# Two block products put between key projection and scores, with the rows for the block sums in another buffer

## The chip, the cores and the metric

The kernel runs on one core of a Trainium2 chip. The metric is device time in microseconds for one execution, from which a median over runs is taken. One execution of the kernel before was recorded by the hardware profiler; all its rows below are in microseconds from the start of its span, unless a column says ns. The engines are named as the profile names them: PE (TensorE, matmuls), DVE (VectorE), ACT (ScalarE), POOL (GpSimd), SP (SyncE, which issues most loads). PE multiplies, DVE and ACT do the element work.

## The reference, cut to what matters

The program is one layer of a hybrid model: 512 tokens, width 1024, float32. Branch A is a gated delta rule, branch B a retention with four heads; then a gate, an output projection and an MLP follow. The change touches branch B alone:

```python
proj = rmsnorm(x, n_mix_pre) @ w_in                     # qb, kb, vb, gb and more are columns of it
qb, kb = rotary(qb, pos), rotary(kb, pos) * 256 ** -0.5 # 4 heads, 256 wide
ob = chunk_retention(qb, kb, vb)                        # scores * decay @ vb, vb 512 wide a head
ob = rmsnorm(ob, norm_b) * silu(gb)
yb = ob.reshape(512, 2048) @ w_br_b                     # 512 rows of ob per head and 512 of w_br_b
```

So `yb` is a sum over the four heads of a (512 tokens x 512) by (512 x 1024) product.

## The kernel before, in words

Every float32 product is made of three matmuls. Each operand is split into a high half, a cast, and a low half, what the cast left over: `whi`/`wlo` for weights (L148 on ACT, L149 on DVE), `kr`, `qr`, `og`, `osum` for the others, each with a cast on ACT (`CAST`) and a subtraction on DVE. The three are high by high, high by low and low by high. A matmul group can start when the high halves are there, and needs the low ones a little later.

Weights come through a ring. SP loads a block of 128x1024 into a `raw` buffer (four of them), ACT and DVE split it into one of three `whi` and three `wlo` buffers, PE uses it. A split waits until PE has used up the buffer that it gets, three blocks back.

Branch B works head by head. The stage of head h runs in this order on PE:

- **Query and key projections**, 48 matmuls of 128x512 each (L93 to L95, two weight blocks for each, results in two banks of `mm` each; there are four `mm` banks in all, taken in turn).
- In the stages of heads 1 to 3, **transposes** (L402, four 128x128 in a group, results in the one bank `tr`) turn the output `o` of the head before, which stands by tokens, into features. `branch_quarters` makes from it the operands of the branch product.
- **Scores** of this head: four groups of keys by queries, 512, 384, 256 and 256 columns wide, into three banks `dl` in turn. DVE takes each from its bank with the decay factors (`sc`), and splits it (`s`).
- **The branch product of the head before**, in `branch_seven`: `o` times the 512x1024 block of `w_br_b`, done with seven half-size block products instead of eight. Three of them, "11", "12" and "22", take quarters of `o` as they are; four, "s1" to "s4", take sums and differences of quarters. Each is 12 matmuls of 128x512. The results are added to `acc` by DVE (for the first head some are copied there by ACT).
- **Values and gates** of this head, again with seven block products (`seven`), and the output `o`.

`rotary` takes a projection's two banks: four products with cosine and sine on DVE (L1541 to L1544, two for each bank), then a difference and a sum (L1545, L1546), then for each the cast (L1548, ACT) and the low half (L1549, DVE). Its result for the keys is `kr`.

Each engine works through its own instructions in a fixed order. That order is made when the program is built, by a scheduler that goes by the order of the code and by priorities (`tc.high_priority`). An instruction that waits holds up everything behind it on its engine.

In the kernel before, `branch_quarters` writes all four transposed feature groups as float32 into a tile `full`, which has the tag `kr`: it takes the same buffer as the keys' result `kr`, so a key cast can write only after everything has read `full`. All the sums and differences, and their halves (`osum`), are made there.

Of the kernel before, what the change touches and what calls it, by code (L numbers as in the profile page):

```python
# [10 lines left out]
F32 = mybir.dt.float32  # L11
# [8 lines left out]
P = 128  # L20
# [43 lines left out]
def hybrid_block_kernel(ctx: ExitStack, tc: tile.TileContext, a: dict, out: bass.AP):  # L64
# [1444 lines left out]
    with tc.tile_pool(name="pb", bufs=1) as pb_:  # L1509
# [41 lines left out]
        def scores(h, rows):  # L1551
# [3 lines left out]
            xq = branch_quarters(h - 1, rows) if rows else None  # L1555
# [4 lines left out]
            if h == 0:  # L1560
                ya_marks.append(ya_partial(3, prev))
            scs = []
# [23 lines left out]
            return scs, xq  # L1586

        def branch_quarters(h, rows):

            full = pb_.tile([P, 4, T], F32, tag="kr", name="full")  # L1590
            og = [act.tile([P, 4, T], F32R, tag="og", name="og") for _ in range(2)]
            sums = [pb_.tile([P, 2, 2, 2, 256], F32R, tag=f"vr{i}", name="osum") for i in range(2)]
            for f in range(4):
                ps = psx.tile([P, 4, P], F32, tag="tr", name="tr", bufs=1)
                for t in range(4):
                    transpose(ps[:, t, :], rows.feature(t, f))
                n = 4 * h + f
# [7 lines left out]
            xq = {}  # L1605

            def halved(name, src, pair):
                nc.scalar.copy(pair[0], src)
                nc.vector.tensor_tensor(pair[1], src, pair[0], ALU.subtract)
                xq[name] = pair  # L1610

            a11, a12, a21, a22 = (part(full, kh, th) for kh, th in ((0, 0), (1, 0), (0, 1), (1, 1)))
            for name, src, kh, th in (("11", a11, 0, 0), ("12", a12, 1, 0)):
                halved(name, src, [part(w, kh, th) for w in og])
            xq["22"] = [part(w, 1, 1) for w in og]
            nc.scalar.copy(xq["22"][0], a22)
            nc.vector.tensor_tensor(xq["22"][1], a22, xq["22"][0], ALU.subtract)
            nc.vector.tensor_tensor(a22, a21, a22, ALU.subtract)
            nc.vector.tensor_tensor(a21, a11, a21, ALU.subtract)
            nc.vector.tensor_tensor(a11, a22, a11, ALU.subtract)  # L1620
            nc.vector.tensor_tensor(a12, a12, a11, ALU.add)
            for i, src in ((2, a11), (1, a22), (3, a21), (4, a12)):
                w = sums[(i - 1) // 2][:, (i - 1) % 2]
                halved(f"s{i}", src, [w[:, 0], w[:, 1]])
            return xq

        def branch_seven(h, xq):
# [22 lines left out]
            a = bank(psx)  # L1650
# [6 lines left out]
            add(0, 0, b)  # L1657
            plus(v, x)
# [3 lines left out]
            c = bank(psm)  # L1662
# [13 lines left out]
        def outputs(h, scs):  # L1676
            vs = [pb_.tile([P, 4, T], F32R, tag=f"vr{i}", name="vr") for i in range(2)]
            gs = pb_.tile([P, 4, T], F32, tag="kr", name="gs")

            def value(t, p):  # L1680
                nc.scalar.copy(vs[0][:, t, :], p)
                nc.vector.tensor_tensor(vs[1][:, t, :], p, vs[0][:, t, :], ALU.subtract)
# [7 lines left out]
            for j in (3, 2, 1, 0):  # L1690
                ps = psx.tile([P, T], F32, tag="dl", name="dl", bufs=3)
                for i in range(j + 1):
                    js = slice((j - i) * P, (j - i + 1) * P)
                    mm3(
                        ps,
                        (scs[i][0][:, js], scs[i][1][:, js]),
                        (vs[0][:, i, :], vs[1][:, i, :]),
                        i == 0,
                        i == j,
                    )  # L1700
                nc.vector.tensor_tensor(o[:, j, :], ps, gs[:, j, :], ALU.mult)
                nc.scalar.activation(tmp("osq"), ps, AF.Square, accum_out=ss[:, j : j + 1])
# [21 lines left out]
        for h in range(4):  # L1724
            scs, xq = scores(h, rows)
# [12 lines left out]
            else:  # L1738
                branch_seven(h - 1, xq)
# [4 lines left out]
        for i in range(2):  # L1744
            ya.append(pb_.tile([P, 2, D], F32, tag=f"vr{i}", name="ya"))
            kept = nc.scalar.dma_start(ya[i], ya_d[:, 2 * i : 2 * i + 2, :])
            gates.append(pb_.tile([P, 2, D], F32, tag=("qr", "kr")[i], name="tb"))

        def gate_b(t, half, src):
            hs = slice(half * 512, half * 512 + 512)  # L1750
            tb = gates[t // 2][:, t % 2, hs]
            nc.scalar.activation(tb, src, AF.Tanh, scale=0.5)
            if t < 2:
                return
            m = acc_rows(t, half)
            nc.vector.scalar_tensor_tensor(m, tb, 1.0, m, ALU.add, ALU.mult)
            nc.vector.tensor_tensor(m, m, ya[t // 2][:, t % 2, hs], ALU.add)
# [10 lines left out]
        for pair in (1, 0):  # L1768
            pss = [[psm.tile([P, T], F32, tag="mm", name="mm") for _ in range(2)] for _ in range(2)]
            for i in range(2):  # L1770
                t = 2 * pair + i
                tt = slice(t * P, (t + 1) * P)
                for half in range(2):
# [7 lines left out]
                    if t < 2:  # L1781
                        rest, total = ya[t // 2][:, t % 2, hs], acc_rows(t, half)
# [334 lines left out]
```

## Time and profile before

| what | value |
|---|---|
| three runs | 1360.79, 1361.19, 1363.46 us |
| median | 1361.19 us |
| the profiled execution | 1362.24 us |
| its span, first to last instruction | 1359.8 us |
| PE busy | 1313.7 us, 97% of the span, 6555 matmuls |
| DVE busy | 971.4 us, 71% |
| ACT busy | 690.4 us, 51% |
| DMA | 231.01 MB, mean 170 GB/s |
| mean granted clock of PE | 0.987 |

The profiled execution has 2.4 us outside its span. A busy PE in this table counts matmuls from start to modelled end, which overlap; what a stage gains by is read from where PE stands idle, or from matmuls that start at a larger distance. The granted clock is the share of full speed that the chip allowed PE.

### The profile page before, as it was taken

The page shows a single profiled execution, that of the slowest core. Times are in us where ns is not written, and L with a number is a line of the kernel's source. Part 1 is how long each engine was busy: PE and PEld are TensorE (multiplying, and loading weights), DVE is VectorE, ACT ScalarE, POOL GpSimd, SP SyncE. Part 2 cuts the span into 40 slices and gives each one's busy share as a digit, 9 for nine tenths or more (in the row PEclk, how much of TensorE's full clock was granted, in tenths as well). Part 3 has the DMA queues.
Part 4 walks back from the last instruction along what each step waited for, and adds up shares of the span by engine and source line. Part 5 has one row for each costly group of instructions (what it writes and reads, how often), then busy time and mean ns, then how long its engine had stood idle before and what let it go on. Part 6 is the DMA issues. An engine that isn't in the chain of part 4 may idle for free.

```text
span 1359.8 us, 17583 instructions
## 1 busy us (share of the span) xinstructions
PE 1313.7 (97%) x6555; PEld 1085.3 (80%) x6555; DVE 971.4 (71%) x1614; ACT 690.4 (51%) x1198; POOL 96.1 (7%) x101
## 2 busy tenths in 40 slices
PE   9999999999999999997997997999999999999997
PEld 7888787888788788886886886888888888888786
DVE  6889767476466578967768868879775746738368
ACT  5783546555433424554554454455355737445364
POOL 2101100000000000010000000000002000001001
PEclk9999999999999999998998998999999999999999
DMA  5337843376675477991494561465629887959735
GB/s 182 135 109 188 199 111 92 96 195 188 179 176 145 93 229 178 267 262 53 150 257 76 149 219 45 140 202 170 224 88 227 223 234 178 268 163 243 211 110 138
DMA packets 118868, 231.01 MB, mean 170 GB/s; under 512 B 7222, under 2 KB 39136, under 8 KB 118272
## 3 DMA queue, kind: packets, MB, share of 16 engines
q1 hardware_dynamic: 98176, 179.85, 40.9%
q0 software_dynamic: 18576, 43.69, 19.8%
q10 hardware_dynamic: 2032, 6.36, 1.3%
q8 instruction: 51, 0.84, 0.2%
q14 instruction: 33, 0.27, 0.1%
HBM read 224.61 MB, written 78.66 MB: 223 GB/s over the span
## 4 chain that ended last, share of the span: by engine, by line
PE 76%; DVE 11%; ACT 6%; DMA 5%; issue 2%; ACTq 0%; DVEq 0%
PE mm L322 16%; PE mm L673 14%; PE dl L322 11%; PE mm L93 7%; PE mm L95 7%; PE mm L94 7%; PE dl L673 5%; DVE wlo L149 3%; DMA raw<-in_w_up_dram 2%; PE dl L93 2%; PE dl L94 1%; PE dl L95 1%; ACT whi L148 1%; PE tr L402 1%; DMA raw<-sums 1%
## 5 line engine op out<-in xcount | busy, mean ns | idle before, releaser
L148 ACT CAST whi<-raw 128x1024 fp32r<-128x1024 f32 x278 | 292.6, 1054 | 369.3 <-PE mm L322 90.1
L149 DVE TENSOR_TENSOR wlo<-raw,whi 128x1024 fp32r<-128x1024 f32 x278 | 339.9, 1223 | 195.0 <-ACT whi L148 194.4
L673 PE MATMUL mm<-actT,whi 128*128 128x512 f32 x448 | 144.5, 403 | 0.0
L322 PE MATMUL mm<-whi,xsum 128*128 128x512 f32 x384 | 120.5, 390 | 0.0
L93 PE MATMUL mm<-hn,whi 128*128 128x512 f32 (+1 forms) x288 | 106.3, 369 | 2.8 <-ACT r L1905 1.8
L95 PE MATMUL mm<-hn,wlo 128*128 128x512 f32 (+1 forms) x288 | 106.2, 369 | 0.5 <-DVE wlo L149 0.5
L94 PE MATMUL mm<-hn,whi 128*128 128x512 f32 (+1 forms) x288 | 105.9, 368 | 0.0
L673 PEld LDWEIGHTS mm<-actT,whi 128*128 128x128 f32 x448 | 80.6, 188 | 14.8
L673 PE MATMUL mm<-actT,wlo 128*128 128x512 f32 x224 | 87.8, 392 | 0.0
L322 PEld LDWEIGHTS mm<-whi,xsum 128*128 128x128 f32 x384 | 71.8, 188 | 14.9
L322 PE MATMUL mm<-wlo,xsum 128*128 128x512 f32 x192 | 74.8, 390 | 0.0
L322 PE MATMUL dl<-whi,ffq 128*128 128x512 f32 x224 | 71.3, 389 | 0.0
L93 PEld LDWEIGHTS mm<-hn,whi 128*128 128x128 f32 x288 | 54.7, 190 | 12.3 <-ACT r L1905 2.0
L95 PEld LDWEIGHTS mm<-hn,wlo 128*128 128x128 f32 x288 | 54.6, 190 | 9.9 <-DVE wlo L149 1.0
L673 PE MATMUL mm<-whi,og 128*128 128x512 f32 x192 | 62.3, 397 | 0.0
L673 PE MATMUL mm<-whi,actT 128*128 128x512 f32 x176 | 60.8, 407 | 1.0 <-DVE qf L907 1.0
L94 PEld LDWEIGHTS mm<-hn,whi 128*128 128x128 f32 x288 | 54.7, 190 | 8.8
L322 PE MATMUL dl<-whi,actT 128*128 128x512 f32 x192 | 61.1, 390 | 0.0
L322 PE MATMUL mm<-whi,ffq 128*128 128x512 f32 x192 | 60.9, 389 | 0.0
L1910 DVE TENSOR_TENSOR ffq<-r,ffq 128x512 fp32r<-128x512 f32 (+1 forms) x64 | 39.3, 623 | 28.0 <-ACT ffq L1910 27.8
L135 POOL DMA_DIRECT2D sums<-in_w_in_dram x28 | 32.7, 1167 | 336.7 <-DMA sums<-in_w_in_dram 336.5
L93 PE MATMUL mm<-actT,whi 128*128 128x512 f32 x128 | 51.5, 402 | 0.0
(426 smaller groups left out, 2877.2 us busy)
## 6 DMA issues: line engine op xcount, KB each, us to landing
raw<-in_w_in_dram SPq DMA_DIRECT2D x95, 512.0 KB, 4.7
raw<-sums SPq DMA_DIRECT2D x70, 512.0 KB, 4.9
raw<-in_w_up_dram SPq DMA_DIRECT2D x36, 512.0 KB, 6.5
sums<-in_w_in_dram SPq DMA_DIRECT2D x32, 512.0 KB, 5.8
sums<-in_w_down_dram SPq DMA_DIRECT2D x32, 512.0 KB, 6.8
sums<-in_w_in_dram POOLq DMA_DIRECT2D x28, 512.0 KB, 7.6
raw<-in_w_down_dram SPq DMA_DIRECT2D x24, 512.0 KB, 4.9
sums<-sums POOLq DMA_DIRECT2D x20, 512.0 KB, 8.2
```

The costliest lines, as they stand in the source:

```text
L93: nc.tensor.matmul(ps, lh, rh, start=first, stop=False)
L94: nc.tensor.matmul(ps, lh, rl, start=False, stop=False)
L95: nc.tensor.matmul(ps, ll, rh, start=False, stop=last)
L135: tc.keep_in_program_order(nc.gpsimd.dma_start(dst, src, accum_op=ALU.add))
L148: nc.scalar.copy(hi[:, :n], raw[:, :n])
L149: nc.vector.tensor_tensor(lo[:, :n], raw[:, :n], hi[:, :n], ALU.subtract)
L322: m = nc.tensor.matmul(pss[t], lhs[i // 2], rhs[i % 2], start=first and k + i == 0, stop=k + i == kts + 1, skip_group_check=not first,)
L402: nc.tensor.transpose(ps, src, ident)
L673: m = tc.keep_in_program_order(nc.tensor.matmul(*args, **kwargs))
L1910: return nc.scalar.copy(dst[0], r), nc.vector.tensor_tensor(dst[1], r, dst[0], ALU.subtract)
```

## The change

Four things are changed, and all concern the stages of heads 1 to 3.

1. **Another buffer.** The tile `full` is gone. Only the two upper feature groups are kept as float32, in `upper`, with a buffer of its own (tag `vr0a`, beside the values). The two lower groups are split straight from the transposes' bank into `og` by `split_from` (L387 on ACT, L388 on DVE). The values' two tiles `vr0`, `vr1` become four half-size tiles; the three other quarters of that room hold the sums. So `kr` no longer waits for readers of `full`.
2. **Two products earlier.** `branch_seven` becomes a generator. Its first part, the products "11" and "12", is called between key projection and scores; the rest runs after the scores. The banks are exchanged for it: the first product's results now go to `mm` banks, those of "s1" and "s4" to `dl` banks.
3. **Sums later.** The sums are made in `branch_sums`, called after the product "12". They start from `upper` alone, and read the lower quarters back from their halves (`xq["22"]`, `xq["12"]`), with an addition or subtraction for each half. "s4" takes the place of the unused quarter in `og`.
4. **Transposes earlier**, by `tc.high_priority(100)`.

Outside the stages, the load of `ya` at the end of branch B is made of four DMAs on ACT's queue instead of two, since it uses the split tiles.

```diff
@@ scores
-            xq = branch_quarters(h - 1, rows) if rows else None
+            parts = branch_quarters(h - 1, rows) if rows else None
...
             if h == 0:
                 ya_marks.append(ya_partial(3, prev))
+            else:
+                branch = branch_seven(h - 1, *parts)
+                next(branch)
             scs = []
...
-            return scs, xq
+            if h:
+                for _ in branch:
+                    pass
+            return scs
@@ branch_quarters
-            full = pb_.tile([P, 4, T], F32, tag="kr", name="full")
             og = [act.tile([P, 4, T], F32R, tag="og", name="og") for _ in range(2)]
-            sums = [pb_.tile([P, 2, 2, 2, 256], F32R, tag=f"vr{i}", name="osum") for i in range(2)]
+            upper = pb_.tile([P, 2, T], F32, tag="vr0a", name="upper")
             for f in range(4):
                 ps = psx.tile([P, 4, P], F32, tag="tr", name="tr", bufs=1)
-                for t in range(4):
-                    transpose(ps[:, t, :], rows.feature(t, f))
-                n = 4 * h + f
-                nc.scalar.activation(
-                    full[:, f, :], ps.rearrange("p t c -> p (t c)"), AF.Copy, scale=nb[:, n : n + 1]
-                )
+                with tc.high_priority(100):
+                    for t in range(4):
+                        transpose(ps[:, t, :], rows.feature(t, f))
+                ps, n = ps.rearrange("p t c -> p (t c)"), 4 * h + f
+                w = nb[:, n : n + 1]
+                if f < 2:
+                    nc.scalar.activation(upper[:, f, :], ps, AF.Copy, scale=w)
+                else:
+                    split_from(ps, og[0][:, f, :], og[1][:, f, :], w)
...
+            xq["s4"] = [part(w, 0, 1) for w in og]
+            a11 = upper[:, :, 0:256]
+            nc.scalar.copy(xq["11"][0], a11)
+            nc.vector.tensor_tensor(xq["11"][1], a11, xq["11"][0], ALU.subtract)
+            return xq, upper
+
+        def branch_sums(xq, upper):
+
+            sums = [pb_.tile([P, 2, 2, 256], F32R, tag=tag, name="osum") for tag in ("vr0b", "vr1a", "vr1b")]
...
+            a11, b = upper[:, :, 0:256], upper[:, :, 256:512]
+            nc.vector.tensor_tensor(b, a11, b, ALU.subtract)
+            halved("s3", b)
+            nc.vector.tensor_tensor(b, b, xq["22"][0], ALU.add)
+            nc.vector.scalar_tensor_tensor(b, b, -1.0, xq["22"][1], ALU.mult, ALU.subtract)
+            halved("s2", b)
+            nc.vector.tensor_tensor(a11, b, a11, ALU.add)
+            halved("s1", a11)
+            nc.vector.tensor_tensor(b, b, xq["12"][0], ALU.add)
+            nc.vector.tensor_tensor(b, b, xq["12"][1], ALU.add)
+            halved("s4", b)
@@ branch_seven
-            a = bank(psx)
+            a = bank(psm)
             times(a, "11", x, True)
             add(0, 0, a, new=True)
...
             times(b, "12", v, True)
             add(0, 0, b)
+            branch_sums(xq, upper)
+            yield
             plus(v, x)
             times(a, "s2", x, False)
...
-            c = bank(psm)
+            c = bank(psx)
             times(c, "s1", w, True)
@@ outputs, and the load of ya at the end
-            vs = [pb_.tile([P, 4, T], F32R, tag=f"vr{i}", name="vr") for i in range(2)]
+            pairs = [[pb_.tile([P, 2, T], F32R, tag=f"vr{i}{x}", name="vr") for x in "ab"] for i in range(2)]
...
-            kept = nc.scalar.dma_start(ya[i], ya_d[:, 2 * i : 2 * i + 2, :])
+            for j in range(2):
+                ya.append(pb_.tile([P, D], F32, tag=f"vr{i}{'ab'[j]}", name="ya"))
+                nc.scalar.dma_start(ya[-1], ya_d[:, 2 * i + j, :])
```

The order of instructions shows where the scheduler put things. First PE at the end of the key projection in the stage of head 2, before the change. `mm<-actT` are the last projection matmuls, `dl<-qr,kr` the scores of this head, `dl<-whi,og` the first matmul of the product "11".

```order
L94 MATMUL mm<-actT,whi 128x512
L95 MATMUL mm<-actT,wlo 128x512
L93 MATMUL dl<-qr,kr 128x512
L94 MATMUL dl<-qr,kr 128x512
L95 MATMUL dl<-qr,kr 128x512
```

The same place after it, where `mm<-whi,og` are the last matmuls of "12".

```order
L322 MATMUL mm<-whi,og 128x512 x2
L322 MATMUL mm<-wlo,og 128x512
L322 MATMUL mm<-whi,og 128x512
L93 MATMUL dl<-qr,kr 128x512
L94 MATMUL dl<-qr,kr 128x512
L93 MATMUL dl<-qr,kr 128x384
L94 MATMUL dl<-qr,kr 128x384
L93 MATMUL dl<-qr,kr 128x256
L94 MATMUL dl<-qr,kr 128x256
L95 MATMUL dl<-qr,kr 128x512
```

The 24 matmuls of two products now stand ahead of the first score. The scores themselves are interleaved: three groups do their first high-by-high and high-by-low matmuls before any does a low-by-high one (L95).

Next DVE in the same stage, before the change, from the keys' last two rotary products (L1543, L1544) to the first score taken from its bank (L1580).

```order
L1543 TENSOR_TENSOR ro<-mm,rope 128x512
L1544 TENSOR_TENSOR ro<-mm,rope 128x512
L149 TENSOR_TENSOR wlo<-raw,whi 128x1024
L1620 TENSOR_TENSOR full<-full 128x2x256
L1609 TENSOR_TENSOR osum<-full,osum 128x512
L1621 TENSOR_TENSOR full<-full 128x2x256
L1609 TENSOR_TENSOR osum<-full,osum 128x512 x3
L1545 TENSOR_TENSOR ro<-ro 128x512
L1546 TENSOR_TENSOR ro<-ro 128x512
L1549 TENSOR_TENSOR kr<-ro,kr 128x512 x2
L1580 TENSOR_TENSOR sc<-dl,dec 128x512
```

And after it, where `acc<-acc,mm` (L1658) adds a half of a finished product to `acc`, the first two of "11" and the next two of "12".

```order
L1543 TENSOR_TENSOR ro<-mm,rope 128x512
L1544 TENSOR_TENSOR ro<-mm,rope 128x512
L149 TENSOR_TENSOR wlo<-raw,whi 128x1024
L1658 TENSOR_TENSOR acc<-acc,mm 128x512 x2
L149 TENSOR_TENSOR wlo<-raw,whi 128x1024
L1658 TENSOR_TENSOR acc<-acc,mm 128x512 x2
L1545 TENSOR_TENSOR ro<-ro 128x512
L149 TENSOR_TENSOR wlo<-raw,whi 128x1024
L1546 TENSOR_TENSOR ro<-ro 128x512
L1549 TENSOR_TENSOR kr<-ro,kr 128x512
L1634 SCALAR_TENSOR_TENSOR upper<-upper,og 128x2x256
L1549 TENSOR_TENSOR kr<-ro,kr 128x512
```

The six rows of sums ahead of L1545 are gone; four additions to `acc` and a second and third weight split stand there or between. Behind them, up to the sums' low halves, come:

```order
L1636 TENSOR_TENSOR upper<-upper 128x2x256
L1583 TENSOR_TENSOR sc<-dl,dec 128x512
L1583 TENSOR_TENSOR sc<-dl,dec 128x384
L1583 TENSOR_TENSOR sc<-dl,dec 128x256
L1583 TENSOR_TENSOR sc<-dl,dec 128x128
L1628 TENSOR_TENSOR osum<-upper,osum 128x512 x2
```

The low halves of "s2" and "s1" (L1628) now follow all four scores. In the stage of head 1, where ACT copies "11" to `acc`, DVE has only the two additions of "12", and they stand behind L1545 and L1546; both low key halves follow them there.

More of the change, by code (lines that the diff above doesn't have):

```diff
@@ L1612, in branch_quarters @@
[L1612 to L1627, printed above, removed]
+            xq = {name: [part(w, kh, th) for w in og] for name, kh, th in (("11", 0, 0), ("12", 1, 0), ("22", 1, 1))}
+            xq["s4"] = [part(w, 0, 1) for w in og]
@@ L1724, in hybrid_block_kernel @@
         for h in range(4):
-            scs, xq = scores(h, rows)
+            scs = scores(h, rows)
             if h == 0:
@@ L1781, in hybrid_block_kernel @@
                     if t < 2:
[L1782 removed]
+                        rest, total = ya[t][:, hs], acc_rows(t, half)
                         nc.vector.tensor_tensor(total, total, pss[i][half], ALU.add)
```

23 lines of the change are left out of this document (11 added, 12 removed).

## The prediction

> **What bounds the kernel now.** I read the busy table first, then the waits of PE, then PE's timeline around the longest wait, then DVE's there, then windows of 3.41 us for the granted clock.
>
> ```profile
> PE 1313.7 (97%) x6555; PEld 1085.3 (80%) x6555; DVE 971.4 (71%) x1614; ACT 690.4 (51%) x1198; POOL 96.1 (7%) x101
> PE dl L93 <- ACT kr L1548: 23.3, 3, 7.8
> PE dl L673 <- ACT vt L1375: 2.9, 1, 2.9
> ```
>
> PE is busy for 97% of the span, so only what PE waits for, or does slowly, is time to be won. One wait towers over the rest: the first score waits for the keys' high half three times, 23.3 us in all; the next one on the list is 2.9 us. PE's timeline shows one of the three, and what follows it:
>
> ```profile
> 622.98 0.39 PE L94 MATMUL mm<-actT,whi 128*128 128x512 f32 x1
> 623.20 0.39 PE L95 MATMUL mm<-actT,wlo 128*128 128x512 f32 x1
> 631.37 0.80 PE L93 MATMUL dl<-qr,kr 128*128 128x512 f32 x1 [7.77 <-ACT kr L1548]
> 631.96 0.63 PE L94 MATMUL dl<-qr,kr 128*128 128x512 f32 x1
> 632.38 0.63 PE L95 MATMUL dl<-qr,kr 128*128 128x512 f32 x1
> 634.69 0.33 PE L93 MATMUL dl<-qr,kr 128*128 128x384 f32 x1
> 634.86 0.33 PE L94 MATMUL dl<-qr,kr 128*128 128x384 f32 x1
> 635.21 0.28 PE L93 MATMUL dl<-qr,kr 128*128 128x256 f32 x1
> 635.33 0.28 PE L94 MATMUL dl<-qr,kr 128*128 128x256 f32 x1
> 639.55 2.72 PE mm L322 x12
> ```
>
> A 512-column matmul starts 0.227 us after the last (2.72 for the 12 of a product) and lasts 0.39, so its result is out 0.16 after the next one's slot. 384 columns take 0.17, 256 take 0.12. Behind the wait, matmuls start 0.43 apart: the clock is down. The windows tell how long:
>
> ```profile
> 347.47:350.88 3.41, 0.60 (x3) 1.00 0.10 36
> 350.88:354.30 3.42, 3.42 (x10) 0.51 0.26 88
> 627.36:630.78 3.42, 0.00 (x0) 0.51 0.43 153
> 630.78:634.19 3.41, 2.83 (x7) 0.50 0.01 2
> 722.94:726.35 3.41, 1.74 (x8) 1.00 0.34 52
> 726.35:729.77 3.42, 0.00 (x0) 1.00 0.31 86
> 729.77:733.18 3.41, 0.74 (x2) 0.50 0.18 67
> 733.18:736.59 3.41, 3.41 (x11) 0.50 0.02 5
> 832.17:835.58 3.41, 1.45 (x4) 0.50 0.02 6
> 835.58:838.99 3.41, 3.41 (x11) 0.50 0.00 0
> ```
>
> Columns: window, its length, PE's busy time, granted clock. Behind a window in which PE was busy for 1.45 us or less stands one at half clock; behind 1.74 us stands a full one. In the three stages PE works 2.83, 0.74 + 3.41 and 1.45 + 3.41 us at half clock, 11.84 in all, and loses half, 5.9. With the waits, the three stages lose **29.2 us**, 9.7 each. That is all there is to win at this place.
>
> Why the keys are late, DVE's timeline tells:
>
> ```profile
> 621.04 0.69 DVE L1541 TENSOR_TENSOR ro<-mm,rope 128x512 f32<-128x512 f32 x1
> 622.24 1.22 DVE L1636 TENSOR_TENSOR raw<-raw 128x1024 f32<-128x1024 f32 x1
> 623.37 0.69 DVE L1619 TENSOR_TENSOR full<-full 128x512 f32<-128x512 f32 x1
> 628.11 1.89 DVE L1609 TENSOR_TENSOR osum<-full,osum 128x512 fp32r<-128x512 f32 x3
> 629.91 0.69 DVE L1545 TENSOR_TENSOR ro<-ro 128x512 f32<-128x512 f32 x1
> 630.51 0.69 DVE L1546 TENSOR_TENSOR ro<-ro 128x512 f32<-128x512 f32 x1
> 631.35 1.29 DVE L1549 TENSOR_TENSOR kr<-ro,kr 128x512 fp32r<-128x512 f32 x2
> ```
>
> DVE never pauses, and does the sums before the keys' difference. A 512-column row takes a slot of 0.60 and is out after 0.69; a 1024-column one 1.13 and 1.22.
>
> **The change, part by part.** All times from here count from the end of the key projection (0 is the slot after its last matmul).
>
> *Sums off the keys' path, two products into the gap.* Products "11" and "12" fill 0 to 5.44. The operands of "11" are early, and its banks are the queries', already read. So the scores can start at 5.44 if the keys are there. They are not, by DVE's new order. I lay it out with the slots above, and with these for ACT and the rest:
>
> ```profile
> 618.32 1.06 ACT L148 CAST whi<-raw 128x1024 fp32r<-128x1024 f32 x1
> 630.69 1.17 ACT L1548 CAST kr<-ro 128x512 fp32r<-128x512 f32 x2 [1.84 <-DVE ro L1545]
> L388 DVE SCALAR_TENSOR_TENSOR og<-tr,vecs,og x4: 743/747/751, 918.0 to 930.5; 128x512 fp32r<-128x512 f32 x4
> ```
>
> Stages of heads 2 and 3, on DVE: the second pair of key products 0.2 to 1.4, the split for "s2" to 2.5, the two additions of "11" to 3.7 (the second half of "11" is out at 2.9), the split for "s1" to 5.1, the first addition of "12" to 5.7, the second to 6.3 ("12" is out at 5.6). Only now L1545, to 7.0; ACT casts it, to 7.64. **First wait: 5.44 to 7.67, 2.23 us.** Six high-half score matmuls (1.03) end at 8.70; the low half comes after the split for "s3" (to 8.03), L1546 (8.63) and L1549 (9.32): **second wait, 0.65**. The fourth score group takes the first group's bank, which DVE reads after the second low half and L1636, until 11.72; PE is there at 11.43: **0.3**. "s2" starts at 12.47 and needs its low half at 12.92; DVE makes it only after the fourth score, at 13.64: **0.75**. Sum 3.95 a stage.
>
> Stage of head 1: ACT makes the copies of "11", so L1545 and L1546 come before all additions and the high keys are there by 5.4. The low half stands behind both additions of "12" and the split for "s1": 0.9. The second low half 0.2, the first bank for the fourth group 0.7 (the low half of "s2" stands ahead of its reader), the low half of "s1" 0.9, since six rows of sums and scores stand ahead. Sum 2.7.
>
> *Transposes earlier.* They move from the key to the query projection. There the first one stands 19 matmuls behind the start, at 599.51 + 4.31 = 603.82, and needs the normed output, which ACT begins at 603.55:
>
> ```profile
> 599.51 0.39 PE L93 MATMUL mm<-actT,whi 128*128 128x512 f32 x1
> 603.55 1.95 ACT L1707 ACTIVATE o<-o,rs_y 128x512 f32<-128x512 f32 x3 [2.42 <-DVE rs_y L383]
> 606.34 0.72 ACT L1707 ACTIVATE o<-o,rs_y 128x512 f32<-128x512 f32 x1
> 610.56 0.44 PE tr L402 x4
> ```
>
> The output is there at 604.3, so PE waits 0.5. I take 0.45 for it and the more frequent switching together; between nothing (the wait took the place of the one for `tr` before) and 1.0.
>
> *DVE and ACT work.* DVE has two rows more a stage (1.2 us) and ACT two casts less (1.0); both stand in the order laid out above, or later beside the values' products, where DVE has time to spare. The split of the values' tiles and two DMAs more at the end I cost at nothing: PE works on a gate's products there; without that cover it is one ACT issue each, under 1 us together. Loads on SP keep their order but for three weight copies, each exchanged with a neighbour: nothing, up to 1 us.
>
> *Sum.* Three times 0.45, 2.7 and twice 3.95 are 11.95 us of new waits. To these comes the clock. The first wait of the stages of heads 2 and 3 has PE idle for 2.1 us, which leaves 1.3 us of work if one window holds all of it, below the 1.45 that brought half clock, and more if it straddles two. One in two, so I count one slow window, with 1.2 us (half of 3.41 at most, less since part of it is waits anyway). 29.2 - 11.95 - 1.2 = **16.0 us gained**. The profiled execution took 1362.24, with 1359.8 of span and 2.4 around it, and would take 1346.2. It stood 1.05 over the median, so I say **1345.2**.
>
> The Trainium skill weighs the clock otherwise: "TensorE: Matmul & The Clock Gate", section "Why this matters for your kernels", wants idle gaps of more than about 3 us before the clock drops. The trace differs: a gap of 2.9 us at 347 was enough. By that page no slow window would be left, and the sum would be 1344.0.
>
> **Rivals.**
>
> *The gain is larger.* The new waits rest on DVE's order and on tenths. Where additions and casts meet PE a little earlier, the four later waits of a stage shrink. Speaking for it: none of them is over 1 us. Without them and without slow windows, the three stages keep 1.35 for the transposes, 0.9, and twice 2.9: 8.0 us; 1361.2 - 29.2 + 8.0 = 1340.0. With no wait left but the transposes', 1333.3. Against it: the first wait hangs on PE itself, as the second addition needs all of "12".
>
> *The clock swings.* Several waits of under 1 us after the first one keep PE under half busy, so that a window follows a window at half clock. For three windows a stage, 1.7 us each, the nine cost 15.4: 1361.2 - 29.2 + 11.95 + 15.4 = 1359.4, no change to speak of. Against it: between the waits lie 1.0 to 1.6 us of work each, and 1.74 us in a window held the clock up. The Trainium skill tells of such a swing on the same page, section "A second HAM failure mode: psum-queue depth-cycling", from short idle times between matmul groups. No window quoted above has one: each half clock stands behind a wait of over 2 us.
>
> *The wait only moves.* The change says that sums come later; if the products "s2" and "s1" then wait for them as the scores did, nothing is won. Ten rows of sums and halves at 0.60 would have to stand between scores and "s2", 6 us a stage, for 18: 1363. The new order has one or two there. That is the 0.75 and 0.9 above.
>
> *Slower.* "12" takes the keys' two banks, which L1541 to L1544 must have read. If DVE arrives late at the keys, "12" and with it the additions, L1545 and the scores move by as much. The three stages pay 4.0 each as laid out, against 9.7; it turns slower by more than can be told from 6.6 us of lateness in each. With 7.5: 1345.2 + 22.5 = 1367.7. For it:
>
> ```profile
> 618.00:624.00 6.00, 5.59 (x25) 4.31 (x23) 6.00 (x10) 2.60 (x4) 0.00 (x0) 1.00 0.00 0
> ```
>
> DVE (the third busy time) has no idle moment around the end of the key projection, and gets two rows more. Against it: the keys' first bank was done at 623.43 - 2.72 + 0.16 = 620.87, and DVE reached L1541 at 621.04, so its lateness came with the sums behind.
>
> **How the numbers follow.** Forecast as laid out, 1341 to 1350: 0.66. A larger gain, 1333 to 1341: 0.16. Clock or moved wait, 1352 to 1363: 0.12, half of it still faster. Slower by DVE's lateness or by something unseen: 0.06. The range takes in most of the larger gain, and upwards two more slow windows (2.4) and 0.3 us on each of the fifteen new waits (4.5): **1338 to 1352**. A change within 0.2%, 2.7 us, is about what a measurement of this kernel can't tell from none. Faster 0.89, same 0.06, slower 0.05.
>
> **What would show it.** In the waits of the changed kernel, "PE dl L93 <- ACT kr" falls from 23.3 to about 4.5, twice some 2.2 and near nothing in the stage of head 1; new rows with low halves come up, `kr` and `osum` on DVE, under 1 us each, and a transpose waiting for `o`, 0.5, three times. DVE's row L1545 stands directly behind the additions of "12" in two stages. The granted clock rises from 0.987 to about 0.993; the windows behind the scores' first wait show 0.50 in at most two stages. The prediction is wrong if the first wait is over 4 us, if DVE reaches L1541 later than the keys' first bank by more than 1 us, or if the rest of the program, above all values and gates behind the branch products, takes longer than before.

## The result and the profile after

The changed kernel takes **1344.99 us** (median of four runs, 1342.42 to 1349.35) against 1361.28 for the kernel before: ratio 0.988, 95% interval 0.985 to 0.991. Run again beside the later experiments it took 1342.43, ratio 0.987 (0.985 to 0.989). The forecast was 1345.2. The profiled execution took 1343.75, with a span of 1341.9.

The busy table of the changed kernel, and the top of the list of what PE waits for within the three stages (total, times, longest):

```profile
PE 1309.0 (98%) x6555; PEld 1078.0 (80%) x6555; DVE 972.6 (72%) x1620; ACT 685.3 (51%) x1192; POOL 96.5 (7%) x101
PE dl L93 <- ACT kr L1548: 4.3, 2, 2.2
PE dl L95 <- DVE kr L1549: 1.5, 3, 0.8
PE mm L322 <- DVE osum L1628: 1.0, 2, 0.5
PE tr L402 <- ACT o L1725: 1.0, 3, 0.3
PE dl L322 <- DVE osum L1628: 0.5, 1, 0.5
```

The wait of the scores for `kr` fell from 23.3 us to 4.3, and small waits came up, for low halves (`kr`, `osum`) and for the output `o` at the transposes. PE's timeline in the stage of head 2, from the last matmul of "12" to the product "s2":

```profile
721.18 0.39 PE L322 MATMUL mm<-whi,og 128*128 128x512 f32 x1
723.74 0.50 PE L93 MATMUL dl<-qr,kr 128*128 128x512 f32 x1 [2.17 <-ACT kr L1548]
725.43 0.80 PE L95 MATMUL dl<-qr,kr 128*128 128x512 f32 x1 [0.37 <-DVE kr L1549]
726.02 0.63 PE L93 MATMUL dl<-qr,kr 128*128 128x512 f32 x1
726.45 0.63 PE L94 MATMUL dl<-qr,kr 128*128 128x512 f32 x1
731.20 0.73 PE L322 MATMUL mm<-whi,osum 128*128 128x512 f32 x2 [0.51 <-DVE osum L1628]
```

And DVE there, where the keys' difference L1545 stands behind the additions of "12":

```profile
718.50 1.28 DVE L1658 TENSOR_TENSOR acc<-acc,mm 128x512 f32<-128x512 f32 x2
720.02 1.23 DVE L149 TENSOR_TENSOR wlo<-raw,whi 128x1024 fp32r<-128x1024 f32 x1 [0.23 <-ACT whi L148]
721.16 1.28 DVE L1658 TENSOR_TENSOR acc<-acc,mm 128x512 f32<-128x512 f32 x2
722.36 0.68 DVE L1545 TENSOR_TENSOR ro<-ro 128x512 f32<-128x512 f32 x1
722.96 1.22 DVE L149 TENSOR_TENSOR wlo<-raw,whi 128x1024 fp32r<-128x1024 f32 x1
724.09 0.68 DVE L1546 TENSOR_TENSOR ro<-ro 128x512 f32<-128x512 f32 x1
```

The key projection's last slot ends at 715.97, so L1545 starts 6.4 behind it, and the score 7.77 behind it. At 726.02 and 726.45 matmuls start 0.43 apart: half clock again, for one window of 3.41 us. The windows of this stage and of the next (window, length, busy times of PE, PEld, DVE, ACT and POOL, granted clock, DMA share, GB/s):

```profile
721.65:725.06 3.41, 1.32 (x6) 1.02 (x6) 3.41 (x6) 1.87 (x3) 0.00 (x0) 1.00 0.98 267
725.06:728.47 3.41, 3.04 (x9) 2.67 (x9) 2.12 (x4) 1.61 (x3) 1.17 (x1) 0.50 0.86 193
817.23:820.64 3.41, 2.10 (x10) 1.40 (x8) 3.17 (x5) 1.56 (x2) 0.00 (x0) 1.00 0.65 171
820.64:824.05 3.41, 2.17 (x10) 1.75 (x11) 3.41 (x6) 1.51 (x3) 0.00 (x0) 1.00 0.97 330
824.05:827.46 3.41, 2.95 (x18) 2.22 (x16) 3.13 (x7) 2.60 (x6) 0.00 (x0) 1.00 0.54 114
```

Behind the wait of head 2, nearly all idle time falls into one window, which has 1.32 us of work; the next one is at half clock. In head 3 the same wait straddles two, 2.10 and 2.17 us of work are left, and the clock stays up.

**Where the time went, by stage.** This table is worked out from PE's timelines. A is query and key projection, B from their end to the first score, C the scores, D from there to the first product of scores with values (in it the rest of the branch product, the values and the gate's products). Each is the sum over the stages of heads 1 to 3. Without any wait A would be 71.8, C 11.5 (3 x 3.82), B 0 and D 171.4, or 16.3 and 155.1 with two products in B.

| kernel | A | B | C | D | sum | median us | ratio to before |
|---|---|---|---|---|---|---|---|
| before | 71.8 | 23.8 | 17.3 | 171.4 | 284.4 | 1361.28 | 1 |
| changed | 73.1 | 21.0 | 17.1 | 157.7 | 268.9 | 1344.99 | 0.988 |
| late sums only | 73.1 | 11.8 | 18.4 | 171.5 | 274.8 | 1349.92 | 0.993 (0.991 to 0.995) |
| products only | 71.8 | 37.9 | 19.7 | 155.1 | 284.5 | 1355.99 | 0.996 (0.994 to 0.998) |
| gap filled | 71.8 | 23.8 | 11.9 | 171.5 | 279.0 | 1354.09 | 0.995 (0.992 to 0.997) |
| late additions | 73.1 | 19.9 | 13.2 | 160.1 | 266.3 | 1342.59 | 0.987 (0.985 to 0.990) |
| "s4" early | 73.1 | 19.9 | 14.7 | 156.6 | 264.3 | 1337.66 | 0.984 (0.982 to 0.987) |
| transposes late | 71.6 | 20.9 | 18.6 | 161.5 | 272.5 | 1347.06 | 0.991 (0.988 to 0.993) |
| keys first | 73.1 | 16.3 | 11.6 | 170.4 | 271.4 | 1349.01 | 0.993 (0.991 to 0.994) |

The sums hardly vary: second profiles gave 284.4 for the kernel before and 268.9 for the changed one. What varies between executions lies outside. In twelve profiles the part ahead of the stages took between 595.0 and 600.2 us, with no order between kernels. Much of that is one place: a wait for `vt` near 347 us, of 0.9 to 3.7 us, and the half clock behind it. The three profiles with no window at half clock there took 595.0, 595.1 and 596.5, the eight with one 596.1 to 599.5, and the one with two 600.2. The two profiled executions of the result differ by 18.5 us: 15.5 in the stages, 3.0 ahead of them (599.5 with such a window, 596.5 without), 0.5 the other way behind, and 0.5 outside the spans. Medians of different kernels are therefore told apart by their ratio's interval, and places by this table. (The kernel before had medians of 1361.28, 1361.7, 1359.48 and 1358.77 beside the four groups of runs; each ratio is to the one run beside it.) The eight times of "late sums only" lie in two groups, five from 1348.4 to 1350.0 at a granted clock of 0.992 or 0.993 and three from 1355.7 to 1357.5 at 0.988 or 0.989; its profile is from the first, so where the second lost its time isn't known.

### The profile page after: what moved, and what is told of

Its sections match the earlier page's. It is cut to its first block, busy times and chain, and to the rows that moved or that the text cites. A ratio compares the mean times of both kernels' runs of the same rounds, so it can differ in the third digit from the quotient of the medians.

```text
span 1341.9 us, 17580 instructions
## 1 busy us (share of the span) xinstructions
PE 1309.0 (98%) x6555; PEld 1078.0 (80%) x6555; DVE 972.6 (72%) x1620; ACT 685.3 (51%) x1192; POOL 96.5 (7%) x101
## 4 chain that ended last, share of the span: by engine, by line
PE 72%; DVE 14%; DMA 6%; ACT 5%; issue 2%; DVEq 0%; ACTq 0%; SPq 0%
PE mm L322 16%; PE mm L673 13%; PE dl L322 11%; PE mm L95 7%; PE mm L94 7%; PE mm L93 7%; PE dl L673 5%; DVE wlo L149 4%; DMA raw<-in_w_in_dram 2%; DMA raw<-sums 2%; ACT whi L148 1%; PE tr L402 1%; PE tr L682 1%; DMA raw<-in_w_up_dram 1%; PE mm L637 1%
## 5 line engine op out<-in xcount | busy, mean ns | idle before, releaser
L95 PE MATMUL mm<-hn,wlo 128*128 128x512 f32 (+1 forms) x288 | 105.5, 366 | 0.5 <-DVE wlo L149 0.5
L673 PEld LDWEIGHTS mm<-actT,whi 128*128 128x128 f32 x448 | 80.6, 188 | 14.7
L322 PEld LDWEIGHTS mm<-whi,xsum 128*128 128x128 f32 x384 | 72.0, 188 | 14.7
L93 PEld LDWEIGHTS mm<-hn,whi 128*128 128x128 f32 x288 | 54.3, 189 | 11.6 <-ACT whi L148 1.5
L95 PEld LDWEIGHTS mm<-hn,wlo 128*128 128x128 f32 x288 | 54.3, 189 | 9.7 <-DVE wlo L149 1.0
```

What stands on the lines that cost most here:

```text
L93: nc.tensor.matmul(ps, lh, rh, start=first, stop=False)
L95: nc.tensor.matmul(ps, ll, rh, start=False, stop=last)
L322: m = nc.tensor.matmul(pss[t], lhs[i // 2], rhs[i % 2], start=first and k + i == 0, stop=k + i == kts + 1, skip_group_check=not first,)
L673: m = tc.keep_in_program_order(nc.tensor.matmul(*args, **kwargs))
```

## The experiments

**The two halves of the change apart.** First the buffer, the late sums and the early transposes, with the products back behind the scores:

```diff
-            else:
-                branch = branch_seven(h - 1, *parts)
-                next(branch)
...
-                for _ in branch:
+                for _ in branch_seven(h - 1, *parts):
...
-            a = bank(psm)
+            a = bank(psx)
...
-            c = bank(psx)
+            c = bank(psm)
```

> The changed kernel with the products "11" and "12" back behind the scores (their banks as before the change); the other buffer, the late sums and the earlier transposes stay. Theory: both halves of the change are needed. Without the sums in the way, DVE reaches the keys' difference 2.5 us behind the key projection (second pair of key products to 1.4, one weight split to 2.5), it is out at 3.2, and its cast at 3.85. PE has nothing else, so the wait of the first score on kr is about 3.9 us in each of the three stages instead of 7.8, with 0.65 + 0.2 for low halves, 0.3 for a bank and 0.45 for a transpose behind it: 5.5 a stage, and again a window at half clock in each, about 1.7. (5.5 + 1.7) x 3 = 21.6 against the 29.2 of before: about 1354, range 1351 to 1357. Rival A, the buffer alone does it: 1345 as with the whole change, with a first wait under 2.5 us. Rival B, without products in the gap nothing is won: 1361.

Measured 1349.92, ratio 0.993 (0.991 to 0.995). PE's wait:

```profile
PE dl L93 <- ACT kr L1548: 11.3, 3, 3.8
PE dl L95 <- DVE kr L1549: 0.4, 1, 0.4
```

The first wait is 3.8 in each stage, as laid out (3.85), with half clock behind each, two windows of it in the stage of head 3. The low halves cost 0.4 in all, not 2.5, so the stages gain more than the 7.6 us expected: 9.6 of the 15.5. The median gained 2.2 us more than the stages did, and so lies below the range expected (1351 to 1357). So rival A is out (buffer, late sums and early transposes don't do it without the products), and B too. The buffer and the late sums were not tried apart.

Then the other half, the products moved and the sums left early:

```diff
+            else:
+                branch = branch_seven(h - 1, xq)
+                next(branch)
...
-            a = bank(psx)
+            a = bank(psm)
...
+            yield
...
-            c = bank(psm)
+            c = bank(psx)
```

> The kernel before with only the products "11" and "12" moved between key projection and scores (banks exchanged); the float32 rows stay in the keys' buffer and all sums stay early. Theory: the products give PE 5.4 us of work, but their four additions to acc and two more weight splits then stand on DVE ahead of the keys' difference, together with the six rows of sums, so that the keys come later by as much: laid out with DVE's slots (0.60 a row, 1.13 a weight split) the high keys are there 13.5 us behind the key projection in the stages of heads 2 and 3 and 11.4 in that of head 1. The first wait is then 8.1, 8.1 and 6.0, 22 us against 23.3 of before, with the half clock behind it as before: about 1360, range 1357 to 1364. Rival, it is the filled gap that pays: 5.4 us less wait in each stage, 16 in all, 1345.

Measured 1355.99, ratio 0.996 (0.994 to 0.998), below the range expected (1357 to 1364). The wait for the keys in all, and DVE in the stage of head 2:

```profile
PE dl L93 <- ACT kr L1548: 21.1, 3, 7.4
724.65 1.22 DVE L149 TENSOR_TENSOR wlo<-raw,whi 128x1024 fp32r<-128x1024 f32 x1
725.78 0.68 DVE L1649 TENSOR_TENSOR acc<-acc,mm 128x512 f32<-128x512 f32 x1
726.52 1.23 DVE L149 TENSOR_TENSOR wlo<-raw,whi 128x1024 fp32r<-128x1024 f32 x1
727.67 0.69 DVE L1626 TENSOR_TENSOR full<-full 128x512 f32<-128x512 f32 x1
729.47 1.89 DVE L1615 TENSOR_TENSOR osum<-full,osum 128x512 fp32r<-128x512 f32 x3
731.28 0.69 DVE L1545 TENSOR_TENSOR ro<-ro 128x512 f32<-128x512 f32 x1
```

PE has 5.44 us of new work in each gap and waits 21.1 us there, hardly less than 23.3. The products brought additions and weight splits with them onto DVE, ahead of L1545. The stages take 284.5, what they took before. The 5.7 us by which the median lay lower are in no stage.

> The kernel with the two products alone once more, unaltered, for a second profile and a second comparison. In its first profile the three stages took 284.5 us, as before the change (284.4 in both of its profiles), though its median lay 5.7 us lower. Theory: the difference is ahead of the stages and by chance; the stages take 284.5 again within 0.5, the part ahead of them comes out between 595 and 600, and the ratio to before lies nearer to 1 than 0.996. Rival, the products alone bring something outside the stages (the part ahead of them shorter by 3 to 4 us again): 595 again and a ratio of 0.996.

Once more: 1356.22, ratio 0.998 (0.997 to 0.9996), stages 283.7, and 598.1 ahead of them. The gain shrank to 2 us, and the rival's other sign, a part of 595 ahead of the stages, didn't come again. That something of the gain is real and lies outside the stages isn't excluded. The profiles show one candidate near 1040 us, behind the stages, where PE waits for `r` in all four. In both profiles of the kernel before, the window there has 1.65 and 1.39 us of PE work, and one at half clock follows; in both of the products alone it has 1.74 and 2.17, and none follows. Whether the change or chance puts the windows so is open.

The halves alone give 9.6 and next to nothing in the stages, together 15.5. The products pay only once the sums are out of DVE's way.

**The clock's share.** The kernel before, with work for PE in the gap and nothing changed for the others:

```diff
+            else:
+                fill = psx.tile([P, T], F32, tag="tr", name="fill", bufs=1)
+                for _ in range(30):
+                    nc.tensor.matmul(fill, xs[0][:, 0, 0:P], xs[0][:, 0, :], start=True, stop=True)
```

> The kernel before with 30 matmuls of 128x512 more in each of the three stages, into the transposes' bank, between key projection and scores; nothing reads their results. They take 6.8 of the 7.8 us for which PE waits there, and change nothing for DVE and ACT. It measures the clock's term alone. Theory: the half clock behind the wait comes from the idle windows. With PE busy the keys come at the same moment (the first score starts as late as before) but the scores run at full clock: 5.9 us less than before, 1355.3, and no window at 0.50 in the three stages. Rival, the half clock has another cause (the scores themselves, or the load that the chip is under): no gain, 1361.

Measured 1354.09, ratio 0.995 (0.992 to 0.997). The wait that is left, and the place in the stage of head 1:

```profile
PE dl L93 <- ACT kr L1548: 2.9, 3, 1.0
621.64 6.96 PE L1565 MATMUL fill<-actT 128*128 128x512 f32 x30
629.57 0.50 PE L93 MATMUL dl<-qr,kr 128*128 128x512 f32 x1 [0.97 <-ACT kr L1548]
630.73 0.40 PE L93 MATMUL dl<-qr,kr 128*128 128x512 f32 x1
630.96 0.40 PE L94 MATMUL dl<-qr,kr 128*128 128x512 f32 x1
```

The score starts 7.93 behind the key projection as before, and the scores take 4.0 us in each stage instead of 5.3 to 6.2. That is 5.4 us, from full clock alone, where 5.9 were reckoned; what the median gained beyond it is in no stage. The half clock came from the idle time.

**What holds the first wait that is left.** The additions of "12" moved behind the scores:

```diff
...
-            add(0, 0, b)
             branch_sums(xq, upper)
             yield
             plus(v, x)
+            add(0, 0, b, prio=0)
...
```

> The changed kernel with one thing more: the additions of the product "12" to acc are written behind the start of the second half of the branch product and lose their priority, so that DVE does them behind the scores. Theory: in the stages of heads 2 and 3 the first wait, 2.17 us, is set by the keys' difference standing behind those two additions. Without them it runs 1.2 us earlier: first wait about 1.0, the wait for the low half 0.6 instead of 0.37, none for osum at "s2" (its low half then stands ahead of the scores on DVE), and no window at half clock. Each stage gains 1.3, and the slow window of the stage of head 2 another 1.3: about 4 us less than the changed kernel, 1341 where that takes 1345. Rival, the wait only moves: what the first wait loses comes back at the low halves or at "s1", the sum of PE's waits on DVE and ACT in the three stages stays at about 8 us, and the time at 1345.

Measured 1342.59, ratio 0.987 (0.985 to 0.990); the stages gain 2.6 on the changed kernel, not 4. DVE, ACT and PE in the stage of head 2, where L1545 starts at 717.83:

```profile
717.83 0.68 DVE L1545 TENSOR_TENSOR ro<-ro 128x512 f32<-128x512 f32 x1
718.28 1.04 ACT L148 CAST whi<-raw 128x1024 fp32r<-128x1024 f32 x1 [1.62 <-PE mm L322]
719.23 1.14 ACT L1548 CAST kr<-ro 128x512 fp32r<-128x512 f32 x2
719.90 0.50 PE L93 MATMUL dl<-qr,kr 128*128 128x512 f32 x1 [1.66 <-ACT kr L1548]
733.98 0.50 PE L322 MATMUL dl<-whi,actT 128*128 128x512 f32 x1 [0.73 <-ACT whi L148]
735.24 0.50 PE L322 MATMUL dl<-wlo,actT 128*128 128x512 f32 x1 [0.76 <-DVE wlo L149]
```

L1545 now starts 5.19 behind the key projection, 1.2 earlier, as expected. But ACT's next weight cast, let go by PE at 718.28, stands ahead of the key cast and takes 0.95 of a slot: the wait falls by 0.5 only. No window at half clock stands in the stages, and the scores take 4.0 us less in all; but D grows by 2.4. The other order of DVE's rows led the scheduler to put two value matmuls into "s4", whose weights are not ready. So both theories had a part: the additions did hold the keys, and more than half of what they gave was held by the next in line.

The waits in "s4" can be taken away. Two things differ from the late additions: the sums of "s4" get priority, and the additions of "12" move once more, from ahead of "s2" to behind "s4":

```diff
+            with tc.high_priority(450):
                 nc.vector.tensor_tensor(b, b, xq["12"][0], ALU.add)
                 nc.vector.tensor_tensor(b, b, xq["12"][1], ALU.add)
                 halved("s4", b)
...
             plus(v, x)
-            add(0, 0, b, prio=0)
...
             times(c, "s4", w, False)
+            add(0, 0, b, prio=0)
```

> The kernel with the late additions of "12", and one thing more: the two sums and the halves for "s4" get priority on DVE. In that kernel's trace two value matmuls stand among those of "s4", and PE waits 0.73 and 0.76 us there for their weights in the stages of heads 2 and 3; with the priority the value matmuls stand behind "22" again. Theory: these waits go, 1.5 us in each of two stages, and what is left in each is the first wait (1.7, now set by a weight cast ahead of the key cast on ACT) and 0.3 for the low half: 3 us less than the kernel with late additions, 1339.6 where that takes 1342.6, and 5 less than the changed kernel. Rival, the weights are late anyway, and the wait only moves behind "22": no gain over the late additions.

That text names the priority alone as the one thing more; the kernel has both.

Measured **1337.66**, ratio 0.984 (0.982 to 0.987), beside 0.987 (0.985 to 0.989) for the changed kernel; the intervals overlap a little, but the stages take 264.3, 4.6 less. This is the fastest version found. The weight waits are gone and D falls by 3.5 against the late additions, so the rival is out; which of the two edits did it was not tried. A new wait of 1.1 for `osum` stands in the stage of head 1, and this time the first wait of head 2 fell into one window of the clock:

```profile
PE dl L322 <- DVE osum L1628: 1.1, 1, 1.1
725.72 0.50 PE L93 MATMUL dl<-qr,kr 128*128 128x512 f32 x1 [1.65 <-ACT kr L1548]
727.34 0.79 PE L95 MATMUL dl<-qr,kr 128*128 128x512 f32 x1 [0.29 <-DVE kr L1549]
723.96:727.37 3.41, 1.46 (x8) 1.06 (x7) 3.41 (x6) 2.62 (x4) 0.00 (x0) 1.00 0.99 279
727.37:730.78 3.41, 3.41 (x10) 3.03 (x11) 1.86 (x4) 0.60 (x1) 1.17 (x1) 0.50 0.83 199
```

**Does the wait only move?** The second half of the keys' rotary product put ahead of all additions (`rest` is 600 for the keys of heads 1 to 3):

```diff
+            with tc.high_priority(rest):
                 nc.vector.tensor_tensor(r[0], r[0], r[1], ALU.subtract)
                 nc.vector.tensor_tensor(r[2], r[2], r[3], ALU.add)
                 for i in range(2):
                     nc.scalar.copy(dst[0][:, i, :], r[2 * i])
                     nc.vector.tensor_tensor(dst[1][:, i, :], r[2 * i], dst[0][:, i, :], ALU.subtract)
```

> The changed kernel with priority for the second half of the keys' rotary product (difference, sum, casts, low halves) in the stages of heads 1 to 3, so that DVE does it ahead of the additions of "11" and "12". Theory: the wait only moves. All of kr is there 4.7 us behind the key projection, so the scores start at 5.44 without a wait and none of the low halves is late; but the second sum for "s2" now stands behind the four additions, three weight splits and the four scores on DVE, 12.6 us behind the key projection in the stages of heads 2 and 3. "s2" could start at 9.4 and waits for the cast of osum until 13.3, 3.9 us, and 0.7 for the low half: 4.6 in a stage against 3.0 in the changed kernel, in one piece long enough for a window at half clock (1.3 to 1.7). About 4 us slower than the changed kernel, 0.990 to 0.991 of before. Rival, DVE has room enough behind the scores: then the first wait's 2.2 us are won in two stages, 4 us faster than the changed kernel, 0.984.

Measured 1349.01, ratio 0.993 (0.991 to 0.994), some 0.5% slower than the changed kernel. Its waits:

```profile
PE mm L322 <- ACT osum L1628: 9.2, 3, 3.5
PE mm L322 <- DVE osum L1629: 1.3, 3, 0.4
729.41 0.50 PE L322 MATMUL mm<-whi,osum 128*128 128x512 f32 x1 [3.52 <-ACT osum L1628]
```

No score waits any more, B and C are at their floor (16.3 and 11.6), and "s2" waits up to 3.5 us for its sum instead. The prediction's rival "the wait only moves" is what happens when the keys go first. In the changed kernel the second sum for "s2" stands among the keys' rows (L1634, between the two rows L1549), and "s2" waits 0.5 at most.

**The transposes' place.** The priority taken off:

```diff
-                with tc.high_priority(100):
-                    for t in range(4):
-                        transpose(ps[:, t, :], rows.feature(t, f))
+                for t in range(4):
+                    transpose(ps[:, t, :], rows.feature(t, f))
```

> The changed kernel without the priority of the transposes: they stand in the key projection again, as before the change. Theory: the earlier place costs PE a wait of 0.33 us in each stage (1.0 in all, by the trace), which goes; but the rows made from the transposes come later on DVE, the second sum of "s2" and its low half now fall behind the keys' low halves, and the wait of "s2" for osum rises from 0.5 to about 1.1 in two stages. Net zero: 1345, within 1 us of the changed kernel. Rival, the two products need the earlier transposes (their operand og is late without): a wait of over 1 us at the first matmul of "11" in each stage, 1348 or more.

Measured 1347.06, ratio 0.991 (0.988 to 0.993), beside 0.987 for the changed kernel. A falls by 1.5, where 1.0 of waiting was expected to go, but the rest grows by 5.1:

```profile
631.12 0.50 PE L95 MATMUL dl<-qr,kr 128*128 128x512 f32 x1 [2.01 <-DVE kr L1549]
741.38 0.49 PE L322 MATMUL dl<-whi,actT 128*128 128x512 f32 x1 [0.73 <-ACT whi L148]
742.63 0.50 PE L322 MATMUL dl<-wlo,actT 128*128 128x512 f32 x1 [0.77 <-DVE wlo L149]
```

Neither theory: the first matmul of "11" doesn't wait, and the waits of "s2" for `osum` stay at 0.5. The loss is in the order that the scheduler makes: a second weight split gets ahead of the keys' low half in the stage of head 1, and value matmuls get among "s4" in the other two, which adds 2.0 to D in each. Another 1.2 us is the clock: a window at half clock stands in the stage of head 3 too.

**Both kernels once more**, for what repeats and what doesn't.

> The changed kernel once more, unaltered, beside the others on one chip, and with a second profile. Theory: 1345, 0.988 of before; the three stages from query projection to the first product of scores and values take 268.9 us together as in its first profile, give or take one window at half clock (1.3 to 1.7 us) in the stage of head 2 or 3; what differs between its runs lies outside them. Rival, the waits themselves vary from run to run: the first waits (2.17 twice) or the low halves come out differently by more than 0.3 us.

> The kernel before once more, unaltered, for a second profile. Theory: the three stages take 284.4 us again within 1 us (waits of 7.8 and half clock behind them), and the part ahead of the first of them, 599.5 us in the first profile, takes between 595 and 600, set by one wait for vt near 347 us and a window at half clock behind it. Rival, it is the stages that differ: then the kernel with the products alone, whose stages took 284.5 in its profile and whose median is 5.7 us lower, has gained in the stages and not by chance ahead of them.

Both theories held. In the changed kernel the same waits came out (4.3, 1.5, 1.0, 1.0, 0.5), the stages took 268.9, with one window at half clock, again in head 2. In the kernel before they took 284.4, and 597.8 ahead of them, with 2.5 us of waiting for `vt` and a window at half clock behind it.

## Why the prediction was right

The time was right, and its terms can be held against the table. They were reckoned as losses against full speed. That the first median came within 0.2 us is in part luck: the same kernel took 1342.43 in the second group of runs, and the part ahead of the stages alone moves by 5 us between profiles.

| term | forecast | measured |
|---|---|---|
| before: waits and half clock in three stages | 29.2 | 29.7 (23.8 in B, 5.9 in C) |
| transposes (A) | 1.35 | 1.25 |
| first waits (B) | 4.5, twice 2.23 | 4.7, twice 2.3 |
| low halves, a bank, one slow window (C) | 4.9 | 5.7 |
| "s1" and "s2" for their low halves (D) | 2.4 | 2.6 |
| gain in the stages | 16.0 | 15.5 |

*What bounds the kernel.* Right: filling the idle time gave 5.4 of the 5.9 us put down to the clock, and taking the sums away shortened each wait for the keys to what DVE's slots had given.

*Sums off the keys' path.* Right to a tenth: L1545 laid out at 6.3 behind the key projection, measured at 6.4, the score at 7.67 and 7.77. The step that carried the forecast was laying out DVE's new order row by row. "It's 5.4 us of work for a 7.8 us gap" would have given the wrong mechanism; that is the products alone, and they gave nothing in the stages.

*Transposes.* Their price was right (0.42 in each stage, of it 0.34 of waiting), but they were put down as a cost only. Without the earlier place the stages take 3.6 us more. That benefit was inside the laid-out order and not seen as theirs.

*The clock.* One slow window was counted in the stages of heads 2 and 3, one in two, and one came, at 1.3 instead of 1.2 us. That it was one, and not none or two, was luck: the two waits are equal, and only the first fell into a single window. The granted clock was forecast at about 0.993, and was 0.992 to 0.997 in the runs. The rule read from the windows (1.45 us of work or less brings half clock, 1.74 doesn't) held in each full-speed window above: 1.32 and 1.46 brought it, 2.10 and 2.17 didn't. The other rule weighed is that of the Trainium skill, page "TensorE: Matmul & The Clock Gate", section "Why this matters for your kernels": no idle gaps of more than about 3 us. Keeping to it was not enough here: two idle times of 2.17 and 0.37 us in one window brought half clock.

*What was costed at nothing.* The part behind the stages took 460.1 to 462.4 us in the five profiles whose `ya` comes in two pieces, and 461.8 to 464.8 in the seven with four. That is some 2 us more where nothing to 1 was reckoned, and a rest that takes longer was one of the prediction's own signs of being wrong. Two small waits show up there, for `keep` (0.5 to 0.8) and for `tb` (0.4), but kernels with two pieces show them too. A wait for a weight cast near 1250 us is longer with four pieces, 0.3 to 2.2 us against at most 1.0. The split loads were not tried by themselves, so the cause is open. Values and gates, which that sign named above all, lie in D, where no more than the 2.6 us of the table was lost.

*The rivals.* A larger gain was there to be had: "s4" early came out at 1337.66, inside the 1333 to 1341 given for it, though by another order and not by luck with the tenths. (The sum given there for a kernel without the later waits, 8.0 us, still holds the first wait for a low half in each stage.) The moved wait exists, in the kernel with the keys first. The clock didn't swing: one window in three stages, in both profiles. The slower rival, DVE late at the keys' first bank, didn't come: with the whole change as with the products alone, DVE reached L1541 some 0.2 us behind the bank. What made the products alone useless is another lateness, of L1545.

## What to carry to other kernels

Work moved into a gap brings its own epilogue with it: count what it puts on the other engines ahead of the thing that the gap waits for, before counting what it fills. Where several engines take turns on a path, lay out the new order with measured slots; when one holder is taken away, look up who is next in line (here ACT's weight cast). A priority that looks like a cost at its own place can hold a whole order together, so try it off before calling it one.

## What was not expected of the hardware

- Half clock needs no long pause. A window of 3.41 us in which PE worked 1.46 us was followed by one at 0.50, at idle times of 1.65 and 0.29 us. The same waits cost 1.3 us more or nothing, by where they fall in the window.
- At full speed the boundary lies between 1.65 and 1.74 us of work: the kernel before has a window with 1.65, near 1040 us, that is followed by half clock. Once the clock is down, more is needed to bring it back. In the kernel with the products alone a window at half clock with 2.41 us is followed by another one; in the kernel before, 2.83 us at half clock was followed by full speed. The first two lines are of the kernel before, the others of the products alone, with the columns as above:

```profile
1040.43:1043.84 3.41, 1.65 (x12) 1.34 (x12) 0.89 (x1) 1.94 (x5) 0.85 (x1) 1.00 0.97 311
1043.84:1047.25 3.41, 3.41 (x10) 2.67 (x9) 2.36 (x5) 3.40 (x10) 0.00 (x0) 0.50 0.94 224
731.72:735.13 3.41, 2.41 (x6) 1.88 (x7) 2.14 (x4) 1.16 (x2) 0.00 (x0) 0.50 0.91 148
735.13:738.54 3.41, 3.41 (x14) 3.31 (x13) 1.62 (x3) 0.96 (x2) 0.00 (x0) 0.50 0.30 46
```

- In twelve profiles of nine kernels, three stages repeat within 0.1 us for the same kernel, while the 595 us ahead of them move by 5. The exception is the kernel with the products alone: 284.5 and 283.7, with 0.8 more in the second between two of the stages.
